# The first group's first value half, multiplied token tile by token tile while the input is read

## The chip, the core and the metric

The kernel runs on one core of one Trainium2 chip. The metric is the device time of one execution in microseconds; three executions of the kernel before give 3003.60, 3006.57 and 3010.51, with a median of 3006.57. A core has a matrix engine (TensorE, PE in the profile), a vector engine (DVE), a scalar engine (ACT), a general engine (POOL) and a queue that issues the transfers (SP). Each engine takes its instructions in the order in which the program lists them, and an instruction that waits holds those behind it.

## What is computed

One layer of a decoder for 2048 tokens of width 1024. The input is normalised, multiplied with one wide matrix and split into seven parts of 512 columns: four for a gated linear recurrence, three (queries, keys, values) for stick-breaking attention. The two results are normalised, joined and projected; a gated feed-forward layer and a gated embedding follow. The change touches only the first lines of this:

```python
u = rmsnorm(h, attn_pre_norm[i])
proj = u @ w_in[i]
hq, hf, hi, hg, sq, sk, sv = jnp.split(proj, splits, axis=-1)
```

where `rmsnorm` scales every token by the inverse root of its mean square and every column by a gain.

## The kernel before

**Tiles.** The 2048 tokens are four groups of 512 (`GT`), a group is four token tiles of 128 rows (`TT`), and the width is eight chunks of 128 (`ND`). A number is kept as a pair, a rounded high part and the remainder, and a product of two pairs is three matmuls (`mm3`, L217 to L219: high by high, and the two mixed ones). The pair is made by two engines: ACT writes the high part, and DVE or POOL subtracts it to get the low one.

**The first group.** `in_norm(0)` loads each token tile in two halves of 512 columns (tag `xt`, eight buffers). `row_rstd` takes the mean square: the first half is squared by ACT (`junk`, L267), the second by DVE (`sq`, L264), and POOL adds them and takes the power -1/2 (L269, L272). DVE scales both halves (L302). `in_u` then transposes everything with TensorE (L312): all eight banks of PSUM are taken, one for each chunk, and the 32 transposes fill them token tile by token tile. Only then is each bank evicted whole: `uh` by ACT with the gain `g_pre` (L328), `ul` by DVE (L329). While the input comes, TensorE turns the identity 36 times (`WARM`, L1199). `build_masks` puts 18 small DVE operations and two of POOL behind this.

**The projection.** `in_proj(0, ...)` goes through the kinds k, q, v; each kind has two halves of 256 columns. `dense` takes two banks of the tag `mm` (three buffers) for a half and walks the eight chunks in pairs; `weight` loads 128 x 512 weights for a pair of chunks into `wr` (four buffers) and splits them (`wh` on ACT, L203, `wl` on DVE and POOL in turn, L204). A half is 96 matmuls for v (256 columns each) and 48 of 512 columns for k or q. Behind each half the banks are evicted and stored: L345 and L346 for k and q, L359 and L360 for v, two copies for each bank.

**The second group** is read by `in_norm(1)`: the same loads (L298) and squares, but both squares and both scalings are on ACT (L267, L304). Its eight `xt` buffers are those of the first group's tiles, so each load waits until TensorE has transposed the tile that held the buffer. Its transposes are woven into the last eight slots of the first group's projection.

**What sets the order.** TensorE's instructions run as the code is written (`manual_schedule`); `weave` interleaves the streams. The other engines' instructions, SP's among them, are ordered at build time by a scheduler with its own idea of times; `tc.high_priority()` moves what stands in it ahead, and `tc.keep_in_program_order` fixes an instruction where the code has it. Two engines that read the same bank of PSUM are put one behind the other.

Of the kernel before, what the change touches and what calls it, by code (L numbers as in the profile page):

```python
# [8 lines left out]
F32 = mybir.dt.float32  # L9
F32R = mybir.dt.float32r  # L10
# [17 lines left out]
EPS = 1e-6  # L28
ROOT = D ** -0.5
WR = 12  # L30
WARM = 36
LEVELS = (1, 2, 4, 8, 16, 32, 64)
BL = 32

# [25 lines left out]
        main.step()  # L60


def build_masks(nc, pool, masks):
# [11 lines left out]
    nc.gpsimd.iota(mi, pattern=[[0, BL]], base=0, channel_multiplier=1)  # L75
    nc.gpsimd.iota(mj, pattern=[[1, BL]], base=0, channel_multiplier=0)
    nc.vector.tensor_single_scalar(mi, mi, BL - 1, op=ALU.bitwise_and)
    nc.vector.tensor_tensor(masks[0], mi, mj, op=ALU.is_equal)
    nc.vector.tensor_tensor(mx, mi, mj, op=ALU.bitwise_xor)
    nc.vector.tensor_tensor(mlt, mi, mj, op=ALU.is_lt)  # L80
    nc.vector.tensor_tensor(mx, mx, mlt, op=ALU.mult)
    for h in LEVELS:
        if h < BL:
            ge, lt = itile("ge"), itile("lt")
            nc.vector.tensor_single_scalar(ge, mx, h, op=ALU.is_ge)
            nc.vector.tensor_single_scalar(lt, mx, 2 * h, op=ALU.is_lt)
            nc.vector.tensor_tensor(masks[h], ge, lt, op=ALU.mult)
# [3 lines left out]
def hybrid_block(  # L91
# [39 lines left out]
    def ctile(name, shape, dt=F32, pool=const):  # L131
        return pool.tile(list(shape), dt, tag=name, name=name)
# [16 lines left out]
    def column(name, src, n, placed=lambda ins: ins):  # L149
        t = ctile(name, (P, n))  # L150
        placed(nc.sync.dma_start(t, src.rearrange("(c p) -> p c", p=P)))
        return t

    g_pre = column("g_pre", attn_pre_norm[0], ND)
    gdif = ctile("gdif", (P, HH))
    lb = ctile("lb", (P, HH))
    oml = ctile("oml", (P, HH))
# [9 lines left out]
    def bank(tag):  # L167
        return ps.tile([P, 512], F32, tag=tag, name=tag, bufs=BANKS[tag])
# [15 lines left out]
    def xt(name="xt"):  # L184
        return fb.tile([P, GT], F32, tag="xt", name=name, bufs=8)
# [73 lines left out]
    def row_rstd(halves, out=None, ss=None, shared=None):  # L259
        if ss is None:  # L260
            ss = const.tile([P, 2], F32, tag="ss", name="ss", bufs=8)
            for j, y in enumerate(halves):
                if j and shared is not None:
                    nc.vector.scalar_tensor_tensor(  # L264
                        shared, y, 1.0 / D, y, op0=ALU.mult, op1=ALU.mult, accum_out=ss[:, j:j + 1])
                else:
                    nc.scalar.activation(junk, y, AF.Square, scale=ROOT, accum_out=ss[:, j:j + 1])  # L267
# [20 lines left out]
    def in_norm(g):  # L288
        toks = []
        for t in range(TT):  # L290
            halves = [xt(), xt()]
            r0 = g * GT + t * P
            for j in range(2):
                if g == 0:
                    with tc.high_priority():
                        nc.sync.dma_start(halves[j], x[r0:r0 + P, j * GT:(j + 1) * GT])
                else:
                    nc.sync.dma_start(halves[j], x[r0:r0 + P, j * GT:(j + 1) * GT])  # L298
            r = row_rstd(halves, shared=att.tile([P, GT], F32, tag="be", name="sq") if g == 0 else None)
            for h in halves:  # L300
                if g == 0:
                    nc.vector.tensor_scalar(h, h, r, None, op0=ALU.mult)  # L302
                else:
                    nc.scalar.activation(h, h, AF.Copy, scale=r)  # L304
            toks.append(halves)
        return toks

    def in_u(toks, u, tags):

        def turn_in(b, c, t):  # L310
            o = c % TT * P
            nc.tensor.transpose(b[:, t * P:(t + 1) * P], toks[t][c // TT][:, o:o + P], ident)  # L312

        whole = len(tags) == ND
        if whole:
            banks = [bank(tag) for tag in tags]
            for t in range(TT):
                for c in range(ND):
                    turn_in(banks[c], c, t)
        for c in range(ND):  # L320
            if whole:
                b = banks[c]
            else:
                b = bank(tags[c % len(tags)])
                for t in range(TT):
                    turn_in(b, c, t)
            hi, lo = operand(wpool, "u", UB)
            nc.scalar.activation(hi, b, AF.Copy, scale=g_pre[:, c:c + 1])  # L328
            nc.vector.scalar_tensor_tensor(  # L329
                lo, b, g_pre[:, c:c + 1], hi.bitcast(F32), op0=ALU.mult, op1=ALU.subtract)  # L330
            u.append((hi, lo))
            yield

    KQV = (("k", 5), ("q", 4), ("v", 6))
    HG = (("hf", 1), ("hq", 0), ("hv", 2), ("hg", 3))

    def in_proj(g, u, kinds):
        def cols(c):
            return lambda k: w_in[k * P:(k + 2) * P, c:c + 256]

        def evict(kind, half, i, b):
            j = 2 * half + i
            if kind in ("q", "k"):
# [41 lines left out]
        for kind, c in kinds:  # L385
            for half in range(2):
# [5 lines left out]
                yield  # L392


    def attention():
        def head_start(g, h):
# [800 lines left out]
    warm = bank("hg")  # L1197
    for i in range(WARM):
        nc.tensor.transpose(warm[:, i % TT * P:(i % TT + 1) * P], ident, ident)  # L1199
# [172 lines left out]
```

## Time and profile before

| quantity | value |
|---|---|
| runs | 3003.60, 3006.57, 3010.51 us; median 3006.57 |
| span of the profiled execution | 3004.9 us |
| mean granted TensorE clock | 0.993 of full |
| DVE, ACT and POOL busy | 68%, 53% and 47% of the span |
| DMA | 602.28 MB, 200 GB/s over the span |

The page gives the profiled execution by its span, from the first to the last instruction; that span is 1.7 us below the median of the runs. In the lists that follow, a row of the timeline has its start and its duration in microseconds, the engine, the line, the operation, what it writes and reads, and in brackets the idle time ahead of it with the instruction or transfer that ended it. Merged rows have a count (x3). A row of the groups has the total, then the mean of one in nanoseconds, then the idle time ahead. Matmuls overlap, so the distance of their starts is what one costs.

### The profile page before, as it was taken

To read this page: it belongs to the slowest core of one execution; us is meant where nothing else is said; L and a number is where in the kernel's file an instruction comes from. 1 tells how busy PE (TensorE), PEld (TensorE's weight loads), DVE (VectorE), ACT (ScalarE), POOL (GpSimd) and SP (SyncE) were. 2 spreads that over 40 slices of the span, in tenths; PEclk is the share of its full clock that TensorE was granted. 3 is DMA by queue.
4 is the path that set the end of the run, shared out by engine and by line. 5 is a ranking of instruction groups with operands and counts; after the bars stand their busy time and mean duration, and the time that the engine had idled before them with its cause. 6 is when DMAs were issued, how large, how long until landed. Compare 5 with 4: busy or idle time off the path is not lost. (4 is left out here: it accounts for less than half of the span.)

```text
span 3004.9 us, 52815 instructions
## 1 busy us (share of the span) xinstructions
PE 2916.8 (97%) x18316; PEld 2428.8 (81%) x18316; DVE 2037.1 (68%) x2865; ACT 1578.5 (53%) x3182; POOL 1402.6 (47%) x1398
## 2 busy tenths in 40 slices
PE   9999999999999999898999999999999999999999
PEld 7888788878787788788777788888888888878777
DVE  3556666677677776766787777655877765656685
ACT  5666756666667666767523243455433323545542
POOL 3344455545556666855523221345722121456653
PEclk9999999999999999999999999999999999999999
DMA  7775665555445444557877677667965555667974
GB/s 221 219 213 155 178 182 164 147 172 165 138 138 163 146 133 139 161 178 254 294 224 248 229 258 252 211 192 223 334 207 168 172 170 178 207 217 231 327 250 161
DMA packets 469419, 602.28 MB, mean 200 GB/s; under 512 B 43168, under 2 KB 277664, under 8 KB 469152
## 3 DMA queue, kind: packets, MB, share of 16 engines
q1 hardware_dynamic: 469152, 598.91, 63.4%
q8 instruction: 144, 2.36, 0.3%
q14 instruction: 123, 1.01, 0.1%
HBM read 439.89 MB, written 158.86 MB: 199 GB/s over the span
## 5 line engine op out<-in xcount | busy, mean ns | idle before, releaser
L822 ACT CAST wh<-wr 128x512 fp32r<-128x512 f32 x600 | 351.3, 618 | 460.1 <-PE mm L218 186.4
L823 POOL TENSOR_TENSOR wl<-wr,wh 128x512 fp32r<-128x512 f32 x256 | 366.1, 1436 | 470.0 <-ACT wh L822 449.8
L445 POOL TENSOR_TENSOR a<-be,ring 128x512 f32<-128x512 f32 (+2 forms) x320 | 319.1, 998 | 418.3 <-DVE ring L441 398.4
L217 PE MATMUL mm<-uh,wh 128*128 128x512 f32 x1168 | 484.5, 415 | 3.3 <-DVE ul L329 1.4
L219 PE MATMUL mm<-uh,wl 128*128 128x512 f32 x1168 | 461.3, 395 | 3.5 <-DVE wl L823 3.5
L218 PE MATMUL mm<-ul,wh 128*128 128x512 f32 x1168 | 459.2, 393 | 0.0
L823 DVE TENSOR_TENSOR wl<-wr,wh 128x512 fp32r<-128x512 f32 x344 | 300.0, 879 | 179.4 <-ACT wh L822 162.2
L441 DVE TENSOR_TENSOR_SCAN ring<-z,ring,be 128x512 f32<-128x512 f32 x192 | 245.6, 1279 | 104.2 <-ACT z L427 101.5
L217 PE MATMUL mm<-wh,uh 128*128 128x256 f32 (+1 forms) x992 | 307.6, 310 | 1.5 <-DVE vv L360 1.5
L218 PE MATMUL mm<-wl,uh 128*128 128x256 f32 (+1 forms) x992 | 292.5, 295 | 0.9 <-POOL wl L823 0.9
L219 PE MATMUL mm<-wh,ul 128*128 128x256 f32 (+1 forms) x992 | 292.6, 295 | 0.0
L219 PEld LDWEIGHTS mm<-uh,wl 128*128 128x128 f32 x1168 | 220.6, 189 | 54.6 <-DVE wl L823 3.9
L217 PEld LDWEIGHTS mm<-uh,wh 128*128 128x128 f32 x1168 | 221.6, 190 | 45.5 <-DVE c L830 1.7
L218 PEld LDWEIGHTS mm<-ul,wh 128*128 128x128 f32 x1168 | 221.9, 190 | 39.5
L458 DVE TENSOR_TENSOR al<-tr,ah 128x512 fp32r<-128x512 f32 (+1 forms) x320 | 192.1, 600 | 82.5 <-ACT ah L456 81.8
L203 ACT CAST wh<-wr 128x512 fp32r<-128x512 f32 x288 | 178.2, 619 | 131.8 <-PE mm L218 76.5
L204 POOL TENSOR_TENSOR wl<-wr,wh 128x512 fp32r<-128x512 f32 x144 | 189.4, 1315 | 102.1 <-ACT wh L203 95.5
L456 ACT CAST ah<-tr 128x512 fp32r<-128x512 f32 (+1 forms) x320 | 167.6, 524 | 108.7 <-PE tr L453 105.1
L426 ACT ACTIVATE be<-z 128x512 f32<-128x512 f32 (+2 forms) x320 | 171.0, 534 | 87.0 <-PE z L424 36.9
L823 POOL TENSOR_TENSOR wl<-s,wh 128x512 fp32r<-128x512 f32 x44 | 71.0, 1618 | 285.4 <-ACT wh L822 282.9
L217 PEld LDWEIGHTS mm<-wh,uh 128*128 128x128 f32 x992 | 190.4, 192 | 9.5 <-issue 1.7
L218 PEld LDWEIGHTS mm<-wl,uh 128*128 128x128 f32 x992 | 190.8, 192 | 6.4 <-POOL wl L823 1.3
(318 smaller groups left out, 7206.7 us busy)
## 6 DMA issues: line engine op xcount, KB each, us to landing
wr<-in_w_gate_up_dram SPq DMA_DIRECT2D x308, 256.0 KB, 3.9
wr<-in_w_in_dram SPq DMA_DIRECT2D x224, 256.0 KB, 3.2
wr<-hid_s SPq DMA_DIRECT2D x154, 256.0 KB, 3.0
wr<-in_w_down_dram SPq DMA_DIRECT2D x110, 256.0 KB, 3.4
wr<-wd_s SPq DMA_DIRECT2D x88, 256.0 KB, 3.2
kt<-k_s SPq DMA_DIRECT2D x80, 256.0 KB, 3.0
vt<-v_s SPq DMA_DIRECT2D x80, 256.0 KB, 3.3
wr<-h_s SPq DMA_DIRECT2D x80, 256.0 KB, 4.2
```

Of the source, the lines that this page charges most:

```text
L203: nc.scalar.copy(hi, src)
L204: (lo_engine or nc.gpsimd).tensor_tensor(lo, src, hi.bitcast(F32), op=ALU.subtract)
L217: nc.tensor.matmul(o, l[0], r[0], start=start, stop=False)
L218: nc.tensor.matmul(o, l[0], r[1], start=False, stop=False)
L219: nc.tensor.matmul(o, l[1], r[0], start=False, stop=stop)
L426: nc.scalar.activation(be[:, :n], z[:, :n], AF.Sigmoid, scale=0.125)
L441: nc.vector.tensor_tensor_scan(r[:, o:o + n][:, ::-1], z[:, :n][:, ::-1], be[:, :n][:, ::-1], init, op0=ALU.mult, op1=ALU.bypass)
L445: nc.gpsimd.tensor_tensor(a[:, :n], be[:, :n], r[:, o + 1:o + n + 1], op=ALU.mult)
L456: nc.scalar.copy(hi[:, lo_c:], tr[:, lo_c:])
L458: nc.vector.tensor_tensor(lo[:, lo_c:], tr[:, lo_c:], hi[:, lo_c:].bitcast(F32), op=ALU.subtract)
L822: nc.scalar.copy(hi, src)
L823: lo_engine.tensor_tensor(lo, src, hi.bitcast(F32), op=ALU.subtract)
```

## The change

The new function `first_values` takes the place of `in_norm(0)` and `in_u` for the first group. It loads token tile 0, two pairs of weights, tile 1, two more pairs of weights, and the last two tiles, and makes the four weight pairs for the first half of v in tiles of tag `a` (`w0h`, `w0l`), which attention uses later. Each token tile is squared, scaled and transposed by itself into two banks (four chunks each), evicted in eight pieces of 128 x 128 by ACT and DVE, and multiplied: `values(t, part)` is 12 matmuls of 256 columns, for four chunks. In TensorE's order the second four chunks of a tile come behind the next tile's transposes. The projection that follows has the second half of v, then k, then q. The masks are built behind its first slots, the warm-up has 48 transposes, and `g_pre` is loaded after the first tile. The first two banks are taken without the counter of `mm_bank`, so banks later in the kernel come in a rotation that is shifted by two.

```diff
-WARM = 36
+WARM = 48
...
-    g_pre = column("g_pre", attn_pre_norm[0], ND)
+    g_pre = ctile("g_pre", (P, ND))
...
+    def first_values(u):
...
+        def scaled(t):
+            ss = const.tile([P, 2], F32, tag="ss", name="ss", bufs=8)
+            sq = att.tile([P, GT], F32, tag="be", name="sq")
+            nc.scalar.activation(junk, xs[t][0], AF.Square, scale=ROOT, accum_out=ss[:, 0:1])
+            nc.vector.scalar_tensor_tensor(
+                sq, xs[t][1], 1.0 / D, xs[t][1], op0=ALU.mult, op1=ALU.mult, accum_out=ss[:, 1:2])
...
+        def turned(t):
+            for j in range(2):
+                b = bank(("z", "av", "z", "tr")[(2 * t + j) % 4])
+                for i in range(TT):
+                    nc.tensor.transpose(b[:, i * P:(i + 1) * P], xs[t][j][:, i * P:(i + 1) * P], ident)
+                for i in range(TT):
+                    c = TT * j + i
+                    o, bi = slice(t * P, (t + 1) * P), b[:, i * P:(i + 1) * P]
+                    hi, lo = u[c]
+                    nc.scalar.activation(hi[:, o], bi, AF.Copy, scale=g_pre[:, c:c + 1])
+                    nc.vector.scalar_tensor_tensor(
+                        lo[:, o], bi, g_pre[:, c:c + 1], hi[:, o].bitcast(F32), op0=ALU.mult, op1=ALU.subtract)
+
+        banks = [bank("mm") for _ in range(2)]
+
+        def values(t, part):
+            for c in range(TT * part, TT * (part + 1)):
+                o = c % 2 * 256
+                mm3(banks[t // 2][:, t % 2 * 256:(t % 2 + 1) * 256], cut(u[c], t),
+                    [w[:, o:o + 256] for w in pairs[c // 2][1:]], c == 0 and t % 2 == 0, c == ND - 1 and t % 2 == 1)
...
+        with tc.high_priority():
+            x_load(0)
+            nc.sync.dma_start(g_pre, attn_pre_norm[0].rearrange("(c p) -> p c", p=P))
+            for k in (0, 2):
+                w_load(k)
+            x_load(1)
+            for k in (4, 6):
+                w_load(k)
+            for t in (2, 3):
+                x_load(t)
+        scaled(0)
+        w_split(0, nc.vector)
+        turned(0)
+        w_split(1, nc.gpsimd)
+        values(0, 0)
+        for t in range(1, TT):
+            scaled(t)
+            turned(t)
+            if t == 1:
+                w_split(2, nc.vector)
+                w_split(3, nc.gpsimd)
+            values(t - 1, 1)
+            values(t, 0)
+        values(TT - 1, 1)
+        return banks
...
-    Stream(in_u(in_norm(0), us[0], ["mm", "mm", "mm", "z", "z", "av", "tr", "hg"])).drain()
+    for i, b in enumerate(first_values(us[0])):
+        in_evict(0)("v", 0, i, b)
...
-    build_masks(nc, att, masks)
-    main = Stream(in_proj(0, us[0], KQV))
+    main = Stream(in_proj(0, us[0], (("v", 6, (1,)), *KQV[:2])))
     weave(main, ND // 2)
...
+    build_masks(nc, att, masks, later)
...
-    weave(main, IN_A - ND - ND // 2)
+    weave(main, IN_A - ND - ND)
```

The rows that follow are the built programs' instructions in their order, with numbered buffers; the line numbers of the changed kernel are its own. First ACT at the start. Before, from the first square of the second group (`xt_403`) on, with the evictions of whole chunks between:

```order
L203 CAST wh_518<-wr_516 128x512
L267 ACTIVATE junk_191,ss_407<-xt_403 128x512
L328 ACTIVATE uh_371<-mm_331,g_pre_170 128x512
L328 ACTIVATE uh_375<-mm_332,g_pre_170 128x512
L328 ACTIVATE uh_379<-mm_333,g_pre_170 128x512
L328 ACTIVATE uh_383<-z_334,g_pre_170 128x512
L328 ACTIVATE uh_387<-z_335,g_pre_170 128x512
L328 ACTIVATE uh_391<-av_336,g_pre_170 128x512
L267 ACTIVATE junk_191,ss_407<-xt_404 128x512
```

Now, the end of the first group's squares and the first evictions (`xt_333` is token tile 3, `z_349` and `av_362` are tile 0's banks, `xt_601` and `xt_602` the second group's first tile):

```order
L407 ACTIVATE junk_190,ss_453<-xt_329 128x512
L407 ACTIVATE junk_190,ss_513<-xt_333 128x512
L426 ACTIVATE uh_288<-z_349,g_pre_170 128x128
L203 CAST wh_657<-wr_655 128x512
L426 ACTIVATE uh_290<-z_349,g_pre_170 128x128
L203 CAST wh_687<-wr_685 128x512
L203 CAST wh_717<-wr_715 128x512
L426 ACTIVATE uh_292<-z_349,g_pre_170 128x128
L267 ACTIVATE junk_190,ss_605<-xt_601 128x512
L426 ACTIVATE uh_294<-z_349,g_pre_170 128x128
L426 ACTIVATE uh_296<-av_362,g_pre_170 128x128
L267 ACTIVATE junk_190,ss_605<-xt_602 128x512
```

All four squares of the first group stand ahead of the first eviction, and the second group's squares now stand between the evictions of single chunks. The same goes on through all four tiles; around tile 1 (`z_399`, `tr_412`) with the second group's next tile (`xt_614`, `xt_615`):

```order
L426 ACTIVATE uh_296<-tr_412,g_pre_170 128x128
L267 ACTIVATE junk_190,ss_618<-xt_614 128x512
L426 ACTIVATE uh_290<-z_399,g_pre_170 128x128
L426 ACTIVATE uh_298<-tr_412,g_pre_170 128x128
L267 ACTIVATE junk_190,ss_618<-xt_615 128x512
L426 ACTIVATE uh_292<-z_399,g_pre_170 128x128
L426 ACTIVATE uh_300<-tr_412,g_pre_170 128x128
L426 ACTIVATE uh_294<-z_399,g_pre_170 128x128
L297 ACTIVATE xt_614<-xt_614,rstd2_623 128x512
```

Two squares stand ahead of tile 1's chunks 1 to 3, and a scaling behind them. Next SP. Before, after the first group's last half tile (`xt_318`):

```order
L296 DMA xt_318<-in_x_dram 128x512
L151 DMA g_pre_170<-in_attn_pre_norm_dram 128x8x1
L212 DMA wr_480<-in_w_in_dram 128x2x256
L212 DMA wr_498<-in_w_in_dram 128x2x256
L212 DMA wr_516<-in_w_in_dram 128x2x256
L212 DMA wr_534<-in_w_in_dram 128x2x256
L298 DMA xt_403<-in_x_dram 128x512
L298 DMA xt_404<-in_x_dram 128x512
```

Now, from the last of the second value half's weights on (`vv_585` is an evicted piece of the values):

```order
L212 DMA wr_745<-in_w_in_dram 128x2x256
L294 DMA xt_601<-in_x_dram 128x512
L294 DMA xt_602<-in_x_dram 128x512
L212 DMA wr_829<-in_w_in_dram 128x2x256
L212 DMA wr_847<-in_w_in_dram 128x2x256
L212 DMA wr_865<-in_w_in_dram 128x2x256
L294 DMA xt_614<-in_x_dram 128x512
L294 DMA xt_615<-in_x_dram 128x512
L294 DMA xt_627<-in_x_dram 128x512
L294 DMA xt_628<-in_x_dram 128x512
L343 DMA v_s0_67<-vv_585 128x512
L343 DMA v_s0_67<-vv_589 128x512
```

The second group's loads now share SP's queue with weights for k and with the stores of the first values. Last TensorE, before, at the end of the transposes (tile 3 is `xt_317` and `xt_318`) and the start of the projection:

```order
L312 MATMUL tr_337<-ident_151,xt_318 128x128
L312 MATMUL hg_338<-ident_151,xt_318 128x128
L217 MATMUL mm_478<-uh_371,wh_482 128x512
L218 MATMUL mm_478<-ul_372,wh_482 128x512
L219 MATMUL mm_478<-uh_371,wl_483 128x512
```

Now, around the transposes of tile 1 (`xt_317`, `xt_318` are that tile here; `uh_294` is chunk 3 and `uh_296` chunk 4, both of tile 0):

```order
L217 MATMUL mm_286<-w0h_315,uh_294 128x256
L218 MATMUL mm_286<-w0l_316,uh_294 128x256
L219 MATMUL mm_286<-w0h_315,ul_295 128x256
L421 MATMUL z_399<-ident_151,xt_317 128x128 x4
L421 MATMUL tr_412<-ident_151,xt_318 128x128 x4
L217 MATMUL mm_286<-w0h_323,uh_296 128x256
```

The transposes of the next tile stand behind the products of a tile's first four chunks.

More of the change, by code (lines that the diff above doesn't have):

```diff
@@ L60, in weave, with build_masks @@
         main.step()
-def build_masks(nc, pool, masks):
+def build_masks(nc, pool, masks, later):
     I32 = mybir.dt.int32
@@ L74, in build_masks @@
     mi, mj, mx, mlt = itile("mi"), itile("mj"), itile("mx"), itile("mlt")
-    nc.gpsimd.iota(mi, pattern=[[0, BL]], base=0, channel_multiplier=1)
-    nc.gpsimd.iota(mj, pattern=[[1, BL]], base=0, channel_multiplier=0)
+    later(nc.gpsimd.iota(mi, pattern=[[0, BL]], base=0, channel_multiplier=1))
+    later(nc.gpsimd.iota(mj, pattern=[[1, BL]], base=0, channel_multiplier=0))
     nc.vector.tensor_single_scalar(mi, mi, BL - 1, op=ALU.bitwise_and)
@@ L293, in in_norm @@
             for j in range(2):
[L294 to L299, printed above, removed]
+                nc.sync.dma_start(halves[j], x[r0:r0 + P, j * GT:(j + 1) * GT])
+            r = row_rstd(halves)
             for h in halves:
[L301 to L304, printed above, removed]
+                nc.scalar.activation(h, h, AF.Copy, scale=r)
             toks.append(halves)
@@ L312, in turn_in @@
             nc.tensor.transpose(b[:, t * P:(t + 1) * P], toks[t][c // TT][:, o:o + P], ident)
-        whole = len(tags) == ND
-        if whole:
-            banks = [bank(tag) for tag in tags]
+        for c in range(ND):
+            b = bank(tags[c % len(tags)])
             for t in range(TT):
[L318 to L326, printed above, removed]
+                turn_in(b, c, t)
             hi, lo = operand(wpool, "u", UB)
@@ L332, in in_u, with in_evict @@
             yield
[L334 to L339, printed above, removed]
+    KQV = (("k", 5, (0, 1)), ("q", 4, (0, 1)), ("v", 6, (0, 1)))
+    HG = (("hf", 1, (0, 1)), ("hq", 0, (0, 1)), ("hv", 2, (0, 1)), ("hg", 3, (0, 1)))
+    def in_evict(g):
         def evict(kind, half, i, b):
@@ L383, in evict, with in_proj, cols @@
                 nc.sync.dma_start(hg_s[g][j], e)
-        for kind, c in kinds:
-            for half in range(2):
+        return evict
+    def in_proj(g, u, kinds):
+        def cols(c):
+            return lambda k: w_in[k * P:(k + 2) * P, c:c + 256]
+        evict = in_evict(g)
+        for kind, c, halves in kinds:
+            for half in halves:
                 for banks in dense(ND, cols(c * 512 + half * 256), u, kind not in ("v", "hv")):
@@ L392, in in_proj, with x_load, w_load, w_split @@
                 yield
+    def first_values(u):
+        order = tc.keep_in_program_order
+        c0 = KQV[2][1] * 512
+        xs, pairs = [], []
+        def x_load(t):
+            xs.append([xt(), xt()])
+            for j in range(2):
+                nc.sync.dma_start(xs[t][j], x[t * P:(t + 1) * P, j * GT:(j + 1) * GT])
+        def w_load(k):
+            raw = wpool.tile([P, 512], F32, tag="wr", name="wr", bufs=4)
+            nc.sync.dma_start(raw.rearrange("p (k n) -> p k n", k=2),
+                              w_in[k * P:(k + 2) * P, c0:c0 + 256].rearrange("(k p) n -> p k n", p=P))
+            pairs.append((raw, *[att.tile([P, GT], F32R, tag="a", name="w0" + s, bufs=8) for s in ("h", "l")]))
+        def w_split(n, e):
+            raw, hi, lo = pairs[n]
+            nc.scalar.copy(hi, raw)
+            e.tensor_tensor(lo, raw, hi.bitcast(F32), op=ALU.subtract)
+        def scaled(t):
[4 more added lines that the diff above has]
+                sq, xs[t][1], 1.0 / D, xs[t][1], op0=ALU.mult, op1=ALU.mult, accum_out=ss[:, 1:2])
+            r = const.tile([P, 1], F32, tag="ssum", name="ssum", bufs=8)
+            order(nc.gpsimd.tensor_scalar(r, ss[:, 0:1], ss[:, 1:2], EPS, op0=ALU.add, op1=ALU.add))
+            out = const.tile([P, 1], F32, tag="rstd2", name="rstd2", bufs=6)
+            order(nc.gpsimd.tensor_tensor(out, r, neghalf, op=ALU.pow))
+            for h in xs[t]:
+                nc.vector.tensor_scalar(h, h, out, None, op0=ALU.mult)
+        def turned(t):
+            for j in range(2):
+                b = bank(("z", "av", "z", "tr")[(2 * t + j) % 4])
[14 more added lines that the diff above has]
+                    [w[:, o:o + 256] for w in pairs[c // 2][1:]], c == 0 and t % 2 == 0, c == ND - 1 and t % 2 == 1)
+        u.extend(operand(wpool, "u", UB) for _ in range(ND))
+        with tc.high_priority():
[23 more added lines that the diff above has]
+        return banks
```

## The prediction

> **What bounds the kernel now.** The page comes first. TensorE is busy for 97% of the span, so whatever the change gains or loses must show as time in which TensorE waits, or runs at half clock.
>
> ```profile
> span 3004.9 us, 52815 instructions
> PE 2916.8 (97%) x18316; PEld 2428.8 (81%) x18316; DVE 2037.1 (68%) x2865; ACT 1578.5 (53%) x3182; POOL 1402.6 (47%) x1398
> ```
>
> Next the timeline of TensorE for the start, which the change rewrites, and for the first half of the values, which it moves (start, duration, operation; in brackets the wait ahead of it).
>
> ```profile
> 1.59 5.51 PE L1199 MATMUL hg<-ident 128*128 128x128 f32 x36 [1.59 <-POOL ident masks.py:199]
> 10.49 0.55 PE L312 MATMUL mm<-ident,xt 128*128 128x128 f32 x3 [3.39 <-DVE xt L302]
> ...
> 18.23 0.80 PE L217 MATMUL mm<-uh,wh 128*128 128x512 f32 x1 [1.42 <-DVE ul L329]
> ...
> 67.07 0.36 PE L217 MATMUL mm<-wh,uh 128*128 128x256 f32 x1
> ...
> 70.03 0.60 PE L312 MATMUL tr<-ident,xt 128*128 128x128 f32 x4
> 70.38 0.36 PE L217 MATMUL mm<-wh,uh 128*128 128x256 f32 x1
> ...
> 80.22 0.36 PE L217 MATMUL mm<-wh,uh 128*128 128x256 f32 x1 [1.54 <-DVE vv L360]
> ```
>
> Projection starts at **18.23**; from there TensorE hardly waits. A quarter of the first value half, 24 products, runs from 67.07 to 70.03, so the half is worth 4 x 2.96 = **11.8 us**, and a product 0.12; four transposes take 0.35 (70.03 to 70.38). So the change pays only if it finishes these products, in its new start, before 18.23 + 11.8 = **30.0**. The clock belongs to the start too: in the table of stretches, columns are TensorE busy, weight load, DVE, ACT, POOL, then the granted clock.
>
> ```profile
> 14.50:16.00 1.50, 0.79 (x7) 0.55 (x6) 1.50 (x3) 0.72 (x2) 0.87 (x1) 0.94 0.79 283
> 16.00:18.00 2.00, 0.81 (x8) 0.57 (x6) 1.97 (x11) 1.92 (x4) 0.00 (x0) 1.00 0.96 343
> 18.00:20.00 2.00, 1.77 (x4) 1.48 (x5) 2.00 (x10) 2.00 (x4) 0.00 (x0) 0.52 0.93 269
> 20.00:21.40 1.40, 1.40 (x5) 1.02 (x5) 1.40 (x6) 1.40 (x5) 0.86 (x2) 0.50 0.89 282
> 21.40:24.00 2.60, 2.60 (x13) 2.14 (x12) 2.32 (x4) 2.06 (x6) 0.73 (x1) 0.98 0.38 133
> ```
>
> Between 14.5 and 18 TensorE was busy 1.60 of 3.5 us, 46%, and the clock then fell to half for some 3.2 us, which cost the projection about 1.6.
>
> **The change part by part.** Work for TensorE is the same but for 12 more warm-up transposes (5.51 / 36 x 12 = 1.8 us). They lie in the 3.39 us wait and cost nothing; without that wait, 1.8. The moved products and the transposes are the same in number and size. What changes is what TensorE waits for: 8 evictions of 128x512 per engine become 32 of 128x128, and ACT's order decides when they run.
>
> *First eviction.* In ACT's order (its rows are in the section on the change) the squares of all four tiles stand ahead of it, so no product can begin before the last token tile has come, whatever the code's order says. The last square, of xt_333, reads the 11th transfer in SP's order. The timeline of ACT before, with the loads on which it waited:
>
> ```profile
> 3.55 0.63 ACT L267 ACTIVATE junk<-xt 128x512 bf16<-128x512 f32 x1 [1.55 <-DMA xt<-in_x_dram]
> 4.09 0.18 ACT L267 ACTIVATION_READ_ACCUMULATOR junk<-xt 128x1 f32 x1
> 6.96 0.63 ACT L267 ACTIVATE junk<-xt 128x512 bf16<-128x512 f32 x1 [2.69 <-DMA xt<-in_x_dram]
> 11.59 2.02 ACT L203 CAST wh<-wr 128x512 fp32r<-128x512 f32 x3 [0.87 <-DMA wr<-in_w_in_dram]
> 14.75 0.63 ACT L267 ACTIVATE junk<-xt 128x512 bf16<-128x512 f32 x1 [1.13 <-DMA xt<-in_x_dram]
> ```
>
> Before, the third transfer landed at 6.96 and the 13th at 14.75: 0.78 each, so the 11th lands near 13.2. A square with its read takes 0.72 (3.55 to 4.27): first eviction at **13.9**.
>
> *An eviction.* The ScalarE and VectorE halves of one bank take turns, as the value evictions do now:
>
> ```profile
> 80.14 0.36 ACT L359 CAST vv<-mm 128x256 fp32r<-128x256 f32 x1
> ```
> ```profile
> 79.65 0.42 DVE L360 TENSOR_TENSOR vv<-mm,vv 128x256 fp32r<-128x256 f32 x1 [3.41 <-ACT vv L359]
> 80.53 0.42 DVE L360 TENSOR_TENSOR vv<-mm,vv 128x256 fp32r<-128x256 f32 x1 [0.46 <-DMA v_s<-vv]
> ```
>
> The second copy of a bank, by ACT at 80.14, starts after the first subtraction, by DVE, ended at 80.07; a turn takes 0.88 (79.65 to 80.53). From the groups by shape (total us and mean ns of one ahead of the second bar):
>
> ```profile
> L426 ACT ACTIVATE be<-z 128x512 f32<-128x512 f32 x224 | 134.0, 598 | 58.4 <-PE z L420 36.2 <-PE z L424 9.6 <-PE av L469 3.1
> L426 ACT ACTIVATE be<-z 128x128 f32<-128x128 f32 x32 | 8.9, 278 | 3.9 <-PE z L424 3.9
> L328 ACT ACTIVATE uh<-mm,g_pre 128x512 fp32r<-128x512 f32 x11 | 7.4, 691 | 0.6 <-PE mm L312 0.6
> L458 DVE TENSOR_TENSOR al<-tr,ah 128x512 fp32r<-128x512 f32 x224 | 152.7, 682 | 71.5 <-ACT ah L456 71.0
> L458 DVE TENSOR_TENSOR al<-tr,ah 128x128 fp32r<-128x128 f32 x32 | 8.8, 276 | 2.5 <-ACT ah L456 2.5
> L329 DVE SCALAR_TENSOR_TENSOR ul<-mm,g_pre,uh 128x512 fp32r<-128x512 f32 x11 | 8.1, 742 | 0.0
> ```
>
> A 128x128 half costs 278 + (691 - 598) = 0.37 on ACT and 276 + (742 - 682) = 0.34 on DVE, a turn with hand-overs 0.8. It lies between 0.55 (278 + 276) and 0.88 (these copies, twice as wide); I take 0.8, nearest to the same shapes.
>
> *The new waits.* In ACT's order the squares and scalings of the **second** group stand between these evictions. Each square waits for a load of x, and each load waits until TensorE has transposed the tile that held its buffer. The DMA queue's own waits show that dependence already (in all, times, longest), but before the change all 32 transposes come first, so it held the loads 0.7 us at most at a time:
>
> ```profile
> SPq L298 <- PE z L312: 1.6, 3, 0.7
> ```
>
> The next row is the time of these loads from issue to landing, asked for by tile; the one behind it, from the timeline of ACT, gives two scalings as 1.33, so 0.66 each:
>
> ```profile
> DMA to landing us min/median/max: 2.8/4.0/6.6
> ```
> ```profile
> 23.09 1.33 ACT L304 ACTIVATE xt<-xt,rstd 128x512 f32<-128x512 f32 x2
> ```
>
> For tile 0 the first such square reads the 17th transfer: 14.75 + 4 x 0.78 = 17.9. With 0.72 for it, 0.8 for the fourth eviction behind it and 0.4 to 0.7 for three products, tile 1 is transposed at about **20**. From there one lap per tile, for in TensorE's order the next tile's transposes stand behind four chunks of this tile's products: four transposes 0.35 to 0.7 (half clock); landing 2.8 to 4.0; hand-over 0.1; on ACT two squares (1.4) and four evictions at 0.27 between banks (1.1); one last turn 0.8; three products 0.4 to 0.7. That is 7.0 to 8.8; I take **8.0**. Tile 2's lap also has two value copies, which wait for twelve products, beside the landing. Three laps end at 44; the last twelve products take 1.4 (0.12 each) to 2.9 at half clock, part of it beside the lap: all values done at **45.5**.
>
> *Credits.* The 1.54 us wait between value halves may go, since ACT has no load to wait for there: half, -0.8. The half clock after 18.23 may or may not come again: half of 1.6, -0.8.
>
> *Costed at nothing.* Masks: 18 small DVE operations and two iotas move behind the values, beside products that need only prefetched weights; uncovered, 18 x 0.175 = 3.2.
>
> ```profile
> L85 DVE TENSOR_SCALAR room<-room 128x32 int32<-128x32 int32 x5 | 0.9, 175 | 0.0
> ```
>
> SP's queue: the value stores and vt loads go ahead of wr_883, whose products come 11.8 us of the second value half and three quarters of a key half (48 products at 0.23 below) later, 20 us. The queries now come last. Attention's first loads of them stand on SP behind the stores of q's first half: four pairs at 1.18 and two landings at 2.8 to 4.0, 10.3 to 12.7 in all. The cover is q's second half and six products of the next projection, 54 products at 0.23, or 12.4; if it falls short, 0.3.
>
> ```profile
> 62.95 0.39 PE L218 MATMUL mm<-ul,wh 128*128 128x512 f32 x1
> 63.18 0.39 PE L219 MATMUL mm<-uh,wl 128*128 128x512 f32 x1
> ```
> ```profile
> 63.49 1.18 SPq L353 DMA_DIRECT2D q_s<-ea  x2
> ```
>
> Two banks fewer are drawn from the rotation, so later banks differ; TensorE's largest wait of that stage is on weights, not banks:
>
> ```profile
> PE z L218 <- POOL wl L204: 10.4, 7, 4.0
> ```
>
> I take 0, within 3 either way.
>
> **Sum:** 45.5 - 30.0 - 1.6 = **+13.9**. Against the profiled span, 3004.9 to 3018.8; the median of the runs, 3006.57, stands 1.7 above the span, so **3020.5**.
>
> **The rivals.**
>
> *Loads land before ACT needs them* (landing hidden). ACT's rows alone: 32 evictions x 0.28, eight squares x 0.72, six scalings x 0.66, three casts x 0.67 (2.02 / 3), two value copies 0.7: 21.4 us from 13.9, plus 1.2 for the last turn and its products: 36.5, so +6.5 less at most 1.54 + 1.6: 3010 to 3013, mostly within 0.2%. Against it: loads can't be issued before the transposes.
>
> *The clock stays full.* The rows say that 46% busy was too little for it. If short gaps did no harm, a lap would lose the slow half of its transposes and products, 0.4, the end 0.2, and the projection would also gain the other half of the 1.6: 13.9 - 1.2 - 0.2 - 0.8 = 11.7, or 3018. [...]
>
> *Faster: evictions keep up with arrival.* If the second group's squares did not hold the evictions, 32 x 0.28 from 13.9 would end at 24.1 with the last turn: -5.9 - 1.6 = -7.5, 2999. It decides wherever the values end before 31.6. For it: DVE and TensorE have room. Against it: ACT's order is fixed, and the second group's rows are in it.
>
> *Slower still:* laps of 8.8, half clock to the end, no credit: 20 + 26.4 + 2.9 - 30.0 = +19.3, with 3 for the later banks 3006.6 + 22.3 = 3028.9.
>
> **How the numbers follow.** Chances: forecast 0.60, hidden loads 0.13, full clock 0.10, slower still 0.09, faster 0.08. Differences of 0.2%, 6 us, are about what a measurement of this kernel can tell from no change. Slower by more: 0.60 + 0.10 + 0.09 = 0.79; within: 0.13; faster: 0.08. The range runs from the hidden loads, 3010 less 1, to the slowest laps, **3009 to 3029**, and leaves out the faster case.
>
> **What would show it.** Right: ACT waiting on loads of x between evictions of 128x128 at about 18, 25, 33 and 41; clock near 0.5 in parts of 15 to 45; second value half starting near 45. Wrong: that half starting before 31.6, or eviction turns far from 0.8. If the start is as worked out and the time is not, the later stages moved, and TensorE's waits after 1300 us would differ.

## The result, and the profile after

The changed kernel takes 3027.25 us in the median (six runs, 3021.31 to 3029.27); the kernel before, run beside it on the same chip, takes 3008.31. The ratio is **1.0066, with a 95% interval of 1.0056 to 1.0077**: about 20 us slower by the ratio, 18.9 by the two medians. The profiled execution, the longest of the six, took 3029.27 us. Its page, in the two lines that answer to those of before:

```profile
span 3027.1 us, 52858 instructions
PE 2927.2 (97%) x18328; PEld 2433.6 (80%) x18328; DVE 2035.8 (67%) x2889; ACT 1584.3 (52%) x3206; POOL 1394.0 (46%) x1398
```

The span grew by 22.2 us, and TensorE's busy time by only 10.4, though the same products run (and 12 warm-up transposes more). The rest is new waiting, and part of the busy time is half clock. Three places carry it: the start, the feed-forward products, and a stretch ahead of these. Attention, behind the start, gives some back.

**The start.** TensorE's timeline after the change (start, duration, operation, in brackets the wait ahead): the first transposes, the first product, the transposes of tiles 1, 2 and 3, and the second half of the values.

```profile
11.42 0.66 PE L421 MATMUL z<-ident,xt 128*128 128x128 f32 x4 [1.64 <-DVE xt L415]
...
13.78 0.39 PE L217 MATMUL mm<-w0h,uh 128*128 128x256 f32 x1 [1.27 <-ACT uh L426]
...
22.98 1.05 PE L421 MATMUL z<-ident,xt 128*128 128x128 f32 x4
...
30.20 0.60 PE L421 MATMUL z<-ident,xt 128*128 128x128 f32 x4
...
36.30 0.60 PE L421 MATMUL z<-ident,xt 128*128 128x128 f32 x4
...
43.58 0.28 PE L217 MATMUL mm<-wh,uh 128*128 128x256 f32 x1
```

The first half of the values ends at 43.58 (`wh` without the 0 is a weight of the second half), where 30.0 would have been break-even. Tile 0 takes 11.6 us (11.42 to 22.98); the laps behind it take 7.2, 6.1 and 7.3. Why tile 0 takes so long is read from the two engines that evict it. ScalarE first, then VectorE:

```profile
13.38 0.35 ACT L426 ACTIVATE uh<-z,g_pre 128x128 fp32r<-128x128 f32 x1
...
16.24 0.37 ACT L426 ACTIVATE uh<-z,g_pre 128x128 fp32r<-128x128 f32 x1 [1.59 <-DVE ul L427]
...
20.50 0.37 ACT L426 ACTIVATE uh<-z,g_pre 128x128 fp32r<-128x128 f32 x1 [2.87 <-DVE ul L427]
```
```profile
12.83 1.90 DVE L415 TENSOR_SCALAR xt<-xt,rstd 128x512 f32<-128x512 f32 x2 [0.46 <-POOL rstd L413]
14.65 0.68 DVE L408 SCALAR_TENSOR_TENSOR sq<-xt 128x512 f32<-128x512 f32 x1
...
15.87 0.34 DVE L427 SCALAR_TENSOR_TENSOR ul<-z,g_pre,uh 128x128 fp32r<-128x128 f32 x1
...
20.13 0.34 DVE L427 SCALAR_TENSOR_TENSOR ul<-z,g_pre,uh 128x128 fp32r<-128x128 f32 x1
```

ScalarE wrote the first high part at 13.38 to 13.73, but the low part of it starts at 15.87: VectorE had the scaling of a later tile and two more squares ahead of it in its queue. The second pair waits in the same way, behind the scaling of tile 3, until 20.13. Each low part holds the next high part of that bank. The waits of the first 62 us say the same in sums (total, times, longest), and the last row says what did *not* hold ScalarE, the landing of the second group's input:

```profile
ACT uh L426 <- DVE ul L427: 5.6, 7, 2.9
...
PE mm L219 <- DVE ul L427: 4.9, 2, 3.1
...
ACT junk L267 <- DMA xt<-in_x_dram: 1.0, 3, 0.5
```

The clock, in the table of stretches with the columns that the prediction names:

```profile
14.50:18.00 3.50, 1.19 (x3) 0.79 (x3) 2.93 (x9) 1.54 (x4) 2.23 (x4) 0.50 0.72 231
...
20.00:24.00 4.00, 3.42 (x12) 2.91 (x13) 2.68 (x8) 2.80 (x9) 0.83 (x2) 0.50 0.59 173
...
27.00:43.50 16.50, 12.86 (x86) 10.80 (x86) 7.47 (x24) 14.15 (x42) 2.58 (x6) 1.00 0.28 97
```

Half clock holds until 24, while tile 0 is stuck; from 27 on the clock is full, though TensorE has gaps. ScalarE is busy for 14.15 of 16.50 us there, the most of all engines: in the laps it sets the pace.

**The way to the feed-forward layer.** By its first and last start, the attention product `z<-kt,q` of before, and that of after:

```profile
L420 PE MATMUL z<-kt,q x640: 221/394/629, 91.7 to 1316.8; 128*128 128x512 f32 x96, 128*128 128x128 f32 x32, 128*128 128x384 f32 x32
```
```profile
L490 PE MATMUL z<-kt,q x640: 222/393/632, 102.5 to 1324.5; 128*128 128x512 f32 x96, 128*128 128x128 f32 x32, 128*128 128x384 f32 x32
```

10.8 us late when attention begins, 7.7 late when it ends. Where the first stretch below begins it is 13.9 late (1895.0 for 1881.1), so another 6.2 us are lost on the way from attention to there. (The mark moves from execution to execution: in the traces of two more kernels that keep the start of before, runs 2 and 8 below, attention begins at 90.0 and 90.2.)

**The feed-forward products.** Three kinds of transposes mark two stretches of it: from the last `hg<-ident,wr` to the first `mm<-ident,c`, and from there to the last `hg<-ident,c`. Before:

```profile
L757 PE MATMUL hg<-ident,wr x64: 270/272/273, 1697.0 to 1881.1; 128*128 128x128 f32 x64
```
```profile
L1096 PE MATMUL mm<-ident,c x64: 270/273/329, 2112.4 to 2788.7; 128*128 128x128 f32 x64
...
L1096 PE MATMUL hg<-ident,c x32: 272/273/329, 2151.2 to 2815.5; 128*128 128x128 f32 x32
```

After:

```profile
L827 PE MATMUL hg<-ident,wr x64: 270/272/273, 1710.9 to 1895.0; 128*128 128x128 f32 x64
```
```profile
L1166 PE MATMUL mm<-ident,c x64: 270/272/328, 2130.1 to 2811.0; 128*128 128x128 f32 x64
...
L1166 PE MATMUL hg<-ident,c x32: 272/273/329, 2169.4 to 2837.8; 128*128 128x128 f32 x32
```

The first stretch goes from 231.3 to 235.1 us, the second from 703.1 to 707.7: together +8.4, a thousand microseconds and more behind the code that was edited. The waits of TensorE between 1895 and 1936 us have one row, which before does not have in that place:

```profile
PE tr L217 <- DVE cu L897: 1.9, 1, 1.9
```

The stretches around it show its whole price:

```profile
1926.00:1929.70 3.70, 3.70 (x17) 2.84 (x16) 3.70 (x7) 1.86 (x3) 0.63 (x1) 1.00 0.77 259
1929.70:1931.80 2.10, 0.20 (x1) 0.00 (x0) 2.10 (x3) 0.27 (x1) 0.92 (x1) 1.00 0.55 150
1931.80:1935.40 3.60, 3.58 (x9) 2.79 (x10) 3.14 (x6) 1.75 (x4) 0.19 (x1) 0.57 0.83 295
```

TensorE stands for 1.92 us and then runs 3.6 us at 0.57 of full clock, another 1.5: 3.4 of the 3.8. The second stretch has the same wait at 2587, of 2.65. The timelines tell why, TensorE's first, then VectorE's:

```profile
1929.51 0.39 PE L219 MATMUL av<-wh,wl 128*128 128x512 f32 x1
1931.82 0.50 PE L217 MATMUL tr<-wh 128*128 128x512 f32 x1 [1.92 <-DVE cu L897]
...
2589.68 0.50 PE L217 MATMUL tr<-wh 128*128 128x512 f32 x1 [2.65 <-DVE cu L897]
```
```profile
1929.41 1.76 DVE L897 TENSOR_TENSOR c<-cu,c 128x512 f32<-128x512 f32 x1
1931.09 0.68 DVE L897 TENSOR_TENSOR cu<-cu,tr 128x512 f32<-128x512 f32 x1
```

The feed-forward layer takes its banks in turn from seven tags (`mm`, `z`, `mm`, `z`, `mm`, `av`, `tr`), and a pass of its gate-and-up part takes fourteen, two full turns, so the last product of every pass has the same tag. (The expectations of runs 1 and 2 call this the rotation of the four `mm` banks.) Before, that was `z`, which has two buffers; shifted by two it is `tr`, which has one. The down part that follows takes `z`, `av`, `tr`, `hg`, and its first `tr` product must wait until VectorE, whose queue is full there, reads the old contents at 1931.09. Before, the same subtraction came as late (1917.20, where the first product of the down part into `z` had begun at 1914.43, in the other buffer), but nothing waited for the bank that it read:

```profile
1917.20 0.68 DVE L827 TENSOR_TENSOR cu<-cu,z 128x512 f32<-128x512 f32 x1
```

### The profile page after: what moved, and what is told of

The parts are those of the page before. It is cut to its first block, busy times and chain, and to the rows that moved or that the text cites. A ratio compares the mean times of both kernels' runs of the same rounds, so it can differ in the third digit from the quotient of the medians.

```text
span 3027.1 us, 52858 instructions
## 1 busy us (share of the span) xinstructions
PE 2927.2 (97%) x18328; PEld 2433.6 (80%) x18328; DVE 2035.8 (67%) x2889; ACT 1584.3 (52%) x3206; POOL 1394.0 (46%) x1398
## 4 chain that ended last, share of the span: by engine, by line
PE 41%; DMA 5%; DVE 5%; issue 4%; POOL 4%; ACT 1%; SPq 0%; POOLq 0%; DVEq 0%; ACTq 0%
PE mm L217 6%; PE mm L219 6%; PE mm L218 6%; PE z L219 4%; PE z L218 4%; PE z L217 4%; PE tr L217 2%; PE tr L219 2%; PE av L217 2%; PE av L219 2%; PE tr L218 2%; PE av L218 2%; DMA wr<-in_w_gate_up_dram 1%; POOL wl L893 1%; DMA wr<-in_w_out_dram 1%
## 5 line engine op out<-in xcount | busy, mean ns | idle before, releaser
L217 PE MATMUL mm<-wh,uh 128*128 128x256 f32 (+1 forms) x960 | 298.2, 311 | 0.0
L218 PE MATMUL mm<-wl,uh 128*128 128x256 f32 (+1 forms) x960 | 284.0, 296 | 0.8 <-POOL wl L893 0.8
L219 PE MATMUL mm<-wh,ul 128*128 128x256 f32 (+1 forms) x960 | 284.0, 296 | 0.0
```

The source lines that it names most:

```text
L217: nc.tensor.matmul(o, l[0], r[0], start=start, stop=False)
L218: nc.tensor.matmul(o, l[0], r[1], start=False, stop=False)
L219: nc.tensor.matmul(o, l[1], r[0], start=False, stop=stop)
```

## The experiments

Each set of kernels is timed in five rounds beside the kernel before, on one chip for the set; its median was 3004.92, 3006.13 and 3005.13 us in the three sets (runs 1 to 4, 5 to 8, and 9). Ratios are to the kernel before.

### 1. The banks put back

```diff
-        banks = [bank("mm") for _ in range(2)]
+        banks = [mm_bank() for _ in range(2)]
```

> The change is kept whole; only the two banks of the first group's values are again taken from the rotation of the four mm banks, so that every later product stands in the bank that it had before the change. Theory (the shift of the rotation by two costs the later part of the span about 11 us): the first attention product stays at about 102 us, the last product of the kernel comes at about 2826 in place of 2837.8, and the time is 3015 to 3019 us. Rival (the later loss comes of the start being late, whatever the banks): the last product stays near 2838 and the time near 3027.

Measured: 3013.26 us, 1.0025 (1.0015 to 1.0036), a little under the expected 3015 to 3019. The first attention product is at 102.1, as late as ever, and the two feed-forward stretches are back at 231.3 (last `hg<-ident,wr` at 1883.3) and 702.8:

```profile
L1166 PE MATMUL mm<-ident,c x64: 270/272/328, 2114.6 to 2790.6; 128*128 128x128 f32 x64
...
L1166 PE MATMUL hg<-ident,c x32: 272/273/329, 2153.6 to 2817.4; 128*128 128x128 f32 x32
```

So one line of the change, which only says where two banks come from, carries more than half of the loss (0.41 of 0.66%). (The last product came at 2817 and not at 2826; attention made up more of the late start in this execution, see below.)

### 2. The shift alone, in the kernel before

```diff
-    mm_count = [0]
+    mm_count = [-2]
```

> The kernel before the change, with nothing altered but the count from which the rotation of the four mm banks starts: minus two in place of nought. Theory (the rotation alone costs about 11 us late in the span): the first attention product stays at 91.7 us, the time is 3016 to 3020 us. Rival (the rotation is worth nothing by itself, it costs only beside a late start): 3005 to 3010 us.

Measured: 3012.71 us, 1.0027 (1.0017 to 1.0037), or 8.1 us (5.1 to 11.1). The start is that of before, and both feed-forward stretches are long, 235.8 (from 1875.0) and 708.3:

```profile
L1096 PE MATMUL mm<-ident,c x64: 270/272/329, 2110.8 to 2792.3; 128*128 128x128 f32 x64
...
L1096 PE MATMUL hg<-ident,c x32: 272/273/328, 2150.4 to 2819.1; 128*128 128x128 f32 x32
```

The shift costs by itself; somewhat less than the 11 us that were expected, and the time lies between the two ranges that were named.

### 3. The second group's rows behind the evictions

```diff
+            pin = tc.keep_in_program_order if g == 1 else (lambda ins: ins)
...
-                nc.scalar.activation(h, h, AF.Copy, scale=r)
+                pin(nc.scalar.activation(h, h, AF.Copy, scale=r))
```

The squares in `row_rstd` are pinned in the same way.

> The change is kept; the squares and scalings on ScalarE of the second group's input are held behind the value evictions of the first group. The prediction's lap (each lap of 8 us carries a 1.4 us pair of these squares and a landing of 2.8 to 4.0): the second half of the values starts 4 to 10 us sooner than 43.6, and the time falls to 3017 to 3023. Rival (VectorE's queue, where the scalings of later tiles and the casts of weights stand ahead of the low parts, holds ScalarE's evictions; the squares only fill that wait): the second half starts at 42 to 44 us and the time stays within 3024 to 3029.

Measured: 3016.84 us, 1.0037 (1.0025 to 1.0049), at the lower end of what was expected. The second half of the values starts at 37.44, 6.1 us sooner, and the first attention product at 97.6. The rival falls: those squares and scalings do cost the laps their time, they do not only fill a wait.

### 4. Everything in the start in a written order

```diff
-        turned(0)
         w_split(1, nc.gpsimd)
+        scaled(1)
+        turned(0)
+        w_split(2, nc.vector)
+        w_split(3, nc.gpsimd)
         values(0, 0)
         for t in range(1, TT):
-            scaled(t)
+            if t + 1 < TT:
+                scaled(t + 1)
             turned(t)
-            if t == 1:
-                w_split(2, nc.vector)
-                w_split(3, nc.gpsimd)
...
-            nc.scalar.activation(junk, xs[t][0], AF.Square, scale=ROOT, accum_out=ss[:, 0:1])
+            order(nc.scalar.activation(junk, xs[t][0], AF.Square, scale=ROOT, accum_out=ss[:, 0:1]))
```

`order` is `tc.keep_in_program_order`, put around all of ScalarE's, VectorE's and GpSimd's instructions in `first_values`; `turned` evicts its two banks by turns.

> As the run with the banks put back, and the second group's rows later; besides the first group's squares, scalings, casts and evictions stand on ScalarE, VectorE and GpSimd in the order in which they are written, and that order is: tile 1's scaling ahead of tile 0's evictions, the last two weight pairs behind tile 0's evictions, and two banks of transposes evicted by turns. Theory (the queue's order sets the laps): ScalarE and VectorE evict two banks side by side, a turn is 0.45 in place of 0.8 us, the start gains 10 to 16 us on the changed kernel (first attention product at 86 to 92 us), and the time is 3000 to 3008. Rival (the turn of an eviction pair is bound by the hand-over between the engines, or by the input's landing): the first attention product at 97 to 103 us, the time 3012 to 3019, which is the bank's part alone.

Measured: 3003.88 us, 0.9998 (0.9989 to 1.0006). The second half of the values starts at 36.01, and the first attention product at 96.3, not at 86 to 92: ScalarE still stood for VectorE, whose queue now had the next tile's scaling ahead of the low part.

```profile
22.36 0.37 ACT L430 ACTIVATE uh<-z,g_pre 128x128 fp32r<-128x128 f32 x1 [2.48 <-DVE ul L431]
```

The time is in the expected range, but 96.3 is nearer to the rival's 97 to 103 than to the theory's 86 to 92. The step that did come out is tile 0: with four chunks' products still ahead of them, tile 1's transposes start at 16.57 and not at 22.98.

### 5. The banks put back for the feed-forward layer alone

```diff
+    mm_count[0] += 2
     mm_tags.append("tr")
```

> The change is kept; the count of the bank rotation is raised by two just before the feed-forward products begin, so that only these get their old banks again. Theory (the shift costs where the last product of a pass stands in the single tr bank, whose eviction the next pass waits for): the wait of a tr product for cu goes from the stretches near 1925 and 2585 us, the stretch from the last hg transposes to the first mm transposes of c is 231 us in place of 235, and the time is 3015 to 3020. Rival (most of the shift's price lies in the stage from 1340 to 1600 us, which keeps the shifted banks): the time stays within 3022 to 3028.

Measured: 3013.71 us, 1.0023 (1.0015 to 1.0032), a little under the expected 3015 to 3020 and the same as with all banks put back. The stretches are 231.3 (from 1888.5) and 703.1, and TensorE has no wait at all in the two places where it waited for `cu`:

```profile
L1166 PE MATMUL mm<-ident,c x64: 270/272/330, 2119.8 to 2796.1; 128*128 128x128 f32 x64
...
L1166 PE MATMUL hg<-ident,c x32: 272/273/329, 2158.5 to 2822.9; 128*128 128x128 f32 x32
```

This places most of the loss in the feed-forward layer and not in the stage from 1340 to 1600 us, which keeps its shifted banks here. A price of 3 us in that stage would not be seen in the time (its trace is taken up below).

### 6. The scalings woven between the evictions

```diff
...
+            evict_u(t, 0)
+            if t + 1 < TT:
+                scaled(t + 1)
+            evict_u(t, 1)
...
```

> As the run with everything pinned; in addition each tile's scaling on VectorE stands between the first and the last four of the previous tile's evictions, the squares are taken two tiles ahead, and the next tile's transposes stand between two pairs of products. Theory (VectorE's order still holds ScalarE in the pinned run: 2.5 us of uh behind ul in tile 1, 1.3 in tile 0): the second half of the values starts at 31 to 34 us in place of 36.0, and the time is 2998 to 3002. Rival (the eviction pairs are bound by their hand-over): it starts at 35 to 37, and the time stays 3002 to 3006.

Measured: 3004.28 us, 0.9994 (0.9986 to 1.0003). The second half starts at 33.33, so the new order, of VectorE's scalings, the squares and the transposes together, was worth 2.7 us more. In the median nothing more is seen: the step is the theory's, the time the rival's. ScalarE's timeline shows what had come next, the cast of a weight for the *second* half, which stands between tile 0's third and fourth eviction and waits for its load:

```profile
14.14 0.62 ACT L203 CAST wh<-wr 128x512 fp32r<-128x512 f32 x1 [3.10 <-DMA wr<-in_w_in_dram]
```

### 7. Two of the three causes removed

The banks put back as in 1, the second group's rows pinned as in 3, and nothing else.

> The change with the banks put back and the second group's squares and scalings held behind the value evictions, nothing pinned in the first group. If the two effects add: 3008 less or more than the 3013.3 of the banks alone by the 5 to 10 us that the second group cost, so 3003 to 3008. If the second group's rows cost only beside the shifted banks: 3011 to 3015.

Measured: 3006.47 us, 1.0004 (0.9994 to 1.0013). By the times the effects add, within the intervals. TensorE's timeline has tile 1 to 3 and the second half of the values at

```profile
22.46 1.05 PE L422 MATMUL z<-ident,xt 128*128 128x128 f32 x4
...
27.28 0.60 PE L422 MATMUL z<-ident,xt 128*128 128x128 f32 x4
...
31.37 0.60 PE L422 MATMUL z<-ident,xt 128*128 128x128 f32 x4
...
36.77 0.28 PE L217 MATMUL mm<-wh,uh 128*128 128x256 f32 x1
```

Laps of 4.8, 4.1 and 5.4 in place of 7.2, 6.1 and 7.3: about 2.1 of a lap was the second group's. Tile 1 still waits until 22.46, so tile 0's delay is not theirs but that of VectorE's queue, as its rows above show.

### 8. The kernel before with the rotation shifted by one

```diff
-    mm_count = [0]
+    mm_count = [-1]
```

> The kernel before, with the rotation of the mm banks started at minus one in place of nought. Theory (a shift costs only where the last feed-forward product of a pass stands in tr): with a shift of one the last product stands in mm and the one before it in tr, so the wait for cu at about 1915 us is absent, the stretch from the last hg transposes to the first mm transposes of c is 231 us, and the time is 3003 to 3010. Rival (the order of before is the only one that fits, any shift costs): the stretch is 234 us or more, the time 3010 to 3016.

Measured: 3005.33 us, 0.9999 (0.9990 to 1.0007); stretches of 231.3 and 703.5 us, and no wait for `cu` there. This shift costs nothing that can be measured. As far as these runs show, a shift costs where it puts the last product of a pass into the tag with one buffer that the next products need early.

### 9. No weight's cast between tile 0's evictions

```diff
...
+            if t < TT - 1:
+                next_half((0, 4)[t - 1])
             if t == 1:
+                next_half(2)
...
```

`next_half` makes the first three weight pairs of the second half in the pinned order, behind the evictions of tiles 1 and 2.

> As the woven run; besides, the casts of the first three weights of the values' second half stand behind the evictions of tiles 1 and 2. In the woven run the first of them stood in ScalarE's queue between the third and the fourth eviction of tile 0 and waited 3.1 us for its load. Theory (that wait set the whole row of laps back): the second half of the values starts at 30 to 31.5 us in place of 33.3, about the break-even of 30.0, the first attention product at 90 to 92 us, and the time is 2999 to 3003, under that of the kernel before. Rival (the loads of the later tiles or of the last two weight pairs are what comes next): it starts at 32.5 to 34 us, and the time stays 3003 to 3006.

Measured: 3003.02 us, 1.0000 (0.9991 to 1.0009). The step came out, even better than expected:

```profile
11.79 0.66 PE L439 MATMUL z<-ident,xt 128*128 128x128 f32 x4 [0.27 <-DVE xt L430]
...
29.36 0.28 PE L221 MATMUL mm<-wh,uh 128*128 128x256 f32 x1
```

Tile 1 is transposed at 11.79, for 16.19 in run 6 and 22.98 in the changed kernel (in runs 6 and 9 its transposes stand behind two chunks' products and not four). The first half ends at 29.36, ahead of the break-even, and the first attention product is at 89.5, 0.5 to 2.2 us sooner than in the three traces with the start of before. The time, 3003.02, lies where the theory's range ends and the rival's begins, and is not under that of the kernel before by anything that can be measured: 2 us in 3005 are 0.07%, less than the interval.

The start in all kernels that change it, in one table:

| kernel | second half of v starts | first attention product | ratio to before |
|---|---|---|---|
| before | 30.0 (break-even) | 91.7 (90.0 and 90.2 in runs 2 and 8) | 1 |
| changed | 43.58 | 102.5 | 1.0066 |
| 1, banks back | 43.22 | 102.1 | 1.0025 |
| 5, banks back for the feed-forward layer | 44.58 | 103.7 | 1.0023 |
| 3, second group later | 37.44 | 97.6 | 1.0037 |
| 7, both (1 and 3) | 36.77 | 96.9 | 1.0004 |
| 4, pinned | 36.01 | 96.3 | 0.9998 |
| 6, woven | 33.33 | 93.5 | 0.9994 |
| 9, no early cast | 29.36 | 89.5 | 1.0000 |

Runs 4, 6 and 9 beat the changed kernel by some 20 us; none is shown to beat the kernel before.

## Why the prediction was right, and where it was wrong

The direction was right, for a reason that holds in the order that the queues had: evictions piece by piece keep TensorE waiting past the break-even (run 9 shows that in another order they need not). 3027.25 lies in the range, near its end, and that is partly luck: the range's end came from laps of 8.8 us and half clock to the last product, and neither happened. The forecast, 3020.5, was too low by about 7 us, because two errors went against each other: the start was 3 us too dear, the later banks were put at nothing.

**Later banks: "I take 0, within 3 either way". This step failed.** The argument was that TensorE's largest wait of the stage from 1340 us was on weights, not banks. It looked at the waits that were there, and at one stage. The shift made a wait where there had been none, in another stage. Its price is 8.1 us alone (run 2, 5.1 to 11.1), 12.3 by the difference of the changed kernel and run 1, and 8.4 by the two stretches in the traces. Seven tags, fourteen products a pass and a fixed order of banks behind them were all to be read in the code. Whether the shift costs more beside the new start than alone the intervals don't settle, but the traces point that way. From attention's last product to the first stretch the three kernels with both take 570.5 us (changed), 567.3 (run 3) and 567.2 (run 5); the other eight, run 2 with the shift alone among them, take 561.7 to 564.4. So 3 to 6 us more seem to be lost there, about what the start alone (7.5) and the shift alone (8.1) leave of the 20. Which wait carries it was not tried and stays open.

**The break-even at 30.0.** It holds: of the kernels with the new start only run 9, at 29.36, begins attention sooner than before.

**First eviction 13.9, the turn 0.8.** The first eviction started at 13.38, and two high parts of one bank start 0.76 to 0.79 apart at the closest, and 0.78 to 0.79 in run 6, where two banks are evicted by turns. In tile 0 the two engines took turns at a bank: VectorE's low parts of 0.34 at 15.87 and 20.13 were followed by ScalarE's next high parts at 16.24 and 20.50, after waits of 1.59 and 2.87 for these reads.

**Tile 1 transposed at 20, held by the second group's first square.** It was 22.98, and the reason was another: with those squares gone it is still 22.46 (run 7). VectorE's queue held tile 0. The prediction quoted ScalarE's order and never looked at VectorE's, where the low parts stand behind the scalings and squares of later tiles. With the orders of ScalarE, VectorE and GpSimd written out it is 16.57 (run 4), and with the finer weave and no early cast 11.79 (run 9). These runs set all three queues right at once: GpSimd takes tile 0's power -1/2 at 6.24 in both, and at 9.83 in the changed kernel, where it stands behind a weight's subtraction. What each queue is worth by itself was not tried.

**Laps of 8.0, "landing 2.8 to 4.0" in each.** They were 7.2, 6.1 and 7.3. The size was near, the make-up was not: ScalarE waited for the input 1.0 us in all three laps together, since it had other work until each load came. So the rival "loads land before ACT needs them" had the mechanism, and the price that the rival left out was VectorE's queue in tile 0. The second group's rows, which the forecast charged with a landing and 1.4 of squares in a lap, were worth 2.1 in all (run 7). Of the signs that it named, ScalarE's waits on loads of x came at 26.7, 33.5 and 39.4, but were 0.2 to 0.5 long, and half clock ended at 24.

**Credits of 1.6 us.** Both went wholly: no wait for `vv` between the value halves, full clock behind 27 us. (Not in every execution: in run 5, with the same start, products start 0.21 us apart from 42.0 to 44.6, and 0.12 apart in the changed kernel's trace.) That is 1.54 + 1.6 = 3.1, and 43.58 - 30.0 - 3.1 = 10.5 against the measured 10.8 at the first attention product. The sum of the start closes to 0.3 us, so the masks, SP's queue and the queries show no cost, though one under the 2 us by which that mark moves would not be seen. The start's +13.9 was 3 too much, 1.9 from the values' end (45.5 for 43.58), 1.5 from the credits.

**From the start to the time.** By run 1 the start alone is worth 7.5 us of time (4.5 to 10.8), by run 5 6.9 (4.5 to 9.6), less than the 10.4 and 12.0 us by which their attention begins late in the traces. Attention gave some of it back: in the changed kernel's trace 10.8 becomes 7.7, in run 1's 10.4 becomes 2.6. Which wait gives it back was not tried.

**The clock.** The rival "the clock stays full" was right for the laps of this trace and wrong for tile 0, where it was at half for about ten microseconds; its 2.2 us could not have been seen in the time.

## What to carry to other kernels

A piece of code that takes its buffers outside a shared rotation moves every later user of that rotation: before costing this at nothing, work out which buffer the last product of each pass gets, how many buffers that tag has, and who needs it next. When work is cut into smaller hand-overs between two engines, read the queues of *both* at build time, since the scheduler may put later tiles' work ahead of the piece that the other engine waits for. And price the best case first: here even a start that is better than break-even brings attention forward by at most 2.2 us, 0.07%, under what can be measured.

## What the runs showed of the hardware

- Half clock followed short waits in places. A wait of 1.92 us was followed by 3.6 us at 0.57 of full clock; a wait of 2.65 us at 2587 by full clock for 1.3 us and then about 4 us at 0.53 to 0.62 (in the rows below, the last figure but two is the clock). Yet from 27 to 43.5 us, 78% busy, it stayed full. Nor does the length of the last pauses decide alone: in the changed kernel, pauses of 1.50, 0.79 and 0.35 between 33 and 42 us were followed by full clock, in run 5 pauses of 1.56, 0.95 and 0.36 by products that start 0.21 apart from 42.0 to 44.6, near half clock, as an estimate from the 0.12 between those starts in the changed kernel at full clock.

```profile
2589.70:2591.00 1.30, 1.30 (x6) 1.08 (x7) 1.27 (x2) 0.00 (x0) 0.00 (x0) 1.00 0.76 254
2591.00:2593.00 2.00, 2.00 (x7) 1.52 (x6) 0.89 (x3) 1.66 (x3) 0.60 (x1) 0.53 0.71 267
2593.00:2595.00 2.00, 2.00 (x7) 1.62 (x6) 1.91 (x2) 0.00 (x0) 0.68 (x1) 0.62 0.46 134
```

- Some of VectorE's operations took about 1 us longer where GpSimd had just begun a subtraction of 128x512: two scalings took 0.88 at 6.84 us in run 9 and 1.90 at 12.83 in the changed kernel, where GpSimd had begun one of 1.28 us at 12.77. The scaling of one half tile took 1.48 at 18.73 and of the other 0.47 at 20.39; GpSimd had begun a subtraction of 1.26 at 18.67. The two long ones stand ahead of tile 0's first and second low part, so about 2 us of tile 0's delay are of this kind, as an estimate from these rows. The subtraction of 1.76 at 1929.41, ahead of the one that freed `tr`, is of that kind too (0.68 for the one behind it; GpSimd's subtraction of 1.55 had begun at 1929.07). Why they took longer no run shows.

```profile
12.77 1.28 POOL L402 TENSOR_TENSOR w0l<-wr,w0h 128x512 fp32r<-128x512 f32 x1
```
